# An output projection done as seven block products in place of eight, on one Trainium2 core

## The chip, the cores and the metric

One NeuronCore of a Trainium2 chip runs one launch of the kernel. The metric is device time in microseconds (us) for the whole step, of the slowest core, which here is the only one. Engines are named as in the profile: PE (TensorE) multiplies matrices, PEld is its weight load, DVE is VectorE, ACT is ScalarE, POOL is GpSimd, SP is SyncE, which only issues DMAs here. Weights are fetched by DMAs that ACT issues. Each engine works through its own instructions in the order in which they stand, and an instruction that waits holds up what stands behind it on its engine.

## The reference

One layer of a hybrid decoder. The prompt has 1024 tokens of width 2048, the decode samples are 8 x 8 = 64 tokens. One input projection gives the columns of 16 heads (6 mLSTM, 6 gated DeltaNet, 4 HGRN2, each 128 wide); each head runs a chunked recurrence; the results go through a norm per head and a gate, then through the output projection and a final norm:

```python
h = _rmsnorm(x, norm_w)
proj = jnp.einsum('bld,de->ble', h, w_in)
...
ha = jnp.concatenate(outs_a, axis=1) * jax.nn.sigmoid(heads(ao, H_A))
hb = jnp.concatenate(outs_b, axis=1)
hc = jnp.concatenate(outs_c, axis=1)
hcat = jnp.concatenate([ha, hb, hc], axis=2)
hcat = hcat * lax.rsqrt(jnp.mean(hcat * hcat, axis=-1, keepdims=True) + EPS)
y = hcat.reshape(bsz, L, MIX) * out_norm_w.astype(f32) * jax.nn.silu(z.astype(f32))
out = jnp.einsum('ble,ed->bld', y.astype(x.dtype), w_out)
return x + out, (st_a[0], st_a[1], st_a[2], st_b, new_conv, st_c)
```

The states of all heads are outputs too. The change touches `y @ w_out`, a product of 1024 (and 64) x 2048 by 2048 x 2048, what feeds it, and what follows it.

## The kernel before

The kernel works in two halves of the prompt, 512 tokens each; the samples ride along with the first. In each half it runs through the heads (`ORDER`). For each head it multiplies the columns of `w_in` with the normed and transposed x, which lies in SBUF in tiles `h00` to `h31`, and then starts the head's scan, its recurrence. These matmuls are called `acc` in the profile, those of the output projection `oacc`.

Products of fp32 precision are made of three fast ones. Every operand is split into `hi` (rounded) and `lo` (the rest), and the product is hi·hi + hi·lo + lo·hi. For weights this is done on the way: `feed_raw` has ACT issue the DMA of a 128 x 512 piece into `wraw` (5 buffers), `feed_split` has ACT cast it to `whi` and DVE subtract to `wlo` (4 buffers each), three pieces ahead of PE. For y, `finish` makes `hi` and `lo` at a head's end and stores both to `y_dram`.

The output projection (lines 1743 to 1802 of before) takes the first half's y from DRAM into the tiles `h..` (`load_y`), as soon as the last columns of the second half have been multiplied. It goes through 4 groups of 512 columns; in each through the 16 heads; and for each head's piece of weights through 4 tiles of 128 tokens (3 matmuls each), and a tile that holds `hi` and `lo` of the 64 samples (2 matmuls). Then it does the same for the second half, without samples. At the end of each group DVE adds the accumulators, which lie in PSUM banks (8 in all), to x; ACT sums squares; POOL multiplies by the final norm's weights. When a token tile has all four groups, `final_norm` scales it and SP stores it.

Work beside the matmuls is written as generators in queues (`scan`, `fin`, `post`, `bg`). `Weave.pump`, called after each handful of matmuls, takes the next step of a queue when its due time, by a rough clock in the code, has come. `drain_queue` steps all queues until the named one is empty, at once, at that point of the program:

```python
def drain(self, *streams):
    while any(not s.done for s in streams):
        heads = [q[0] for q in self.queues.values() if q]
        due = min(s.due for s in heads)
        self.clock.t["T"] = max(self.clock.t["T"], due)
        self.pump()
```

Names in the profile: `pan`, `pa`, `pkh`, `puh`, `poh` are the PE steps of an HGRN2 head's scan, in that order; `X`, `Ex`, `hkd`, `hqd` are made for it by POOL. The last head, C3, is such a one, and its scan runs into the output projection. `yd<-y` and `s<-yd` move y of a head through DRAM in `finish`; `Bb<-db` brings rows for the triangular solves of the gated DeltaNet heads.

Of the kernel before, what the change touches and what calls it, by code (L numbers as in the profile page):

```python
# [6 lines left out]
F32 = mybir.dt.float32  # L7
F32R = mybir.dt.float32r
# [5 lines left out]
P = 128  # L14
# [131 lines left out]
class Weave:  # L146
    def __init__(self, clock):
        self.clock = clock
        self.queues = {"scan": [], "fin": [], "post": [], "bg": []}
# [37 lines left out]
OUT_UNITS = ([(cg, range(5)) for cg in range(4)], [(cg, range(4)) for cg in range(3)] + [(3, range(2)), (3, range(2, 4))])  # L187
# [3 lines left out]
def hybrid_step(ctx, tc, i, o):  # L191
# [51 lines left out]
    def o_raw(k, cg):  # L243
        raw = wp.tile([P, 512], F32, tag="wraw", name="wraw", bufs=5)
        WDMA(raw, i["w_out"][0, P * k:P * (k + 1), 512 * cg:512 * (cg + 1)])
        return raw

# [95 lines left out]
    for units in OUT_UNITS:  # L343
        for cg, _ in units:
            for k in range(NK):
                pieces.append((o_raw, k, cg))
# [256 lines left out]
    y_dram = [dp.tile([NH, P, w], F32R, name=f"y{w}") for w in (2 * NSAMP + 2 * HALF, 2 * HALF)]  # L603
# [233 lines left out]

    def finish(half, head, outs, ssq, scale, zs):
# [30 lines left out]
        yield  # L869
        yhi, ylo = zs.bitcast(F32R), y.bitcast(F32R)  # L870
# [4 lines left out]
        d = y_dram[half.index][head].bitcast(F32)  # L875
        for part, t in enumerate((yhi, ylo)):
            t = t.bitcast(F32)
            at_ = 2 * NSAMP if half.first else 0
            DMA(d[:, at_ + HALF * part:at_ + HALF * (part + 1)], t[:, 0:HALF])
            if half.first:  # L880
                DMA(d[:, NSAMP * part:NSAMP * (part + 1)], t[:, HALF:WS])
# [90 lines left out]
    def mlstm_scan(half, h, kT, qT, vT, tho, zs, nm, em, st):  # L972
# [118 lines left out]
        weave.add("fin", finish(half, h, hxs, ssq, 0.25, zs))  # L1091
# [60 lines left out]
    def gdn_scan(half, h, ck_, cq, cv, zs, Gb, eG, bb, st):  # L1152
# [242 lines left out]
        weave.add("fin", finish(half, HA + h, hxs, ssq, 1.0, zs))  # L1395
# [22 lines left out]
    def hgrn_scan(half, h, kT, lf, qT, vT, zs, st):  # L1418
# [152 lines left out]
        weave.add("fin", finish(half, HA + HB + h, hxs, ssq, 0.25, zs))  # L1571
# [91 lines left out]
    def load_y(half, g):  # L1663
        w = y_dram[half.index].shape[-1]
        yT[half.index][g] = [hp.tile([P, 2, w], F32R, tag=f"h{g}{part}", name=f"y{g}{part}") for part in (0, 1)]
        for q in range(4):
            DMA(yT[half.index][g][q // 2][:, q % 2].bitcast(F32), y_dram[half.index][4 * g + q].bitcast(F32))

    def y_block(half, k, n, part):

        at_ = HALF * part + P * n
        return yT[half.index][k // 4][k % 4 // 2][:, k % 2, at_:at_ + P]

    hB, yT = {}, [{}, {}]
    for half, groups in zip(halves, group_lists):
# [4 lines left out]
        for n, group in enumerate(groups):  # L1680
# [5 lines left out]
            if half.first and n == 6:  # L1686
                weave.add("bg", prep_B())
            after = None
            if n == len(groups) - 1:
# [3 lines left out]
                else:  # L1693
                    after = lambda g: load_y(halves[0], g)
# [12 lines left out]

    ys_flat = o["y_sample"].rearrange("b t d -> (b t) d")
    tags = ["a", "b", "c", "d", "e", "f", "g", "h", "j", "a", "b", "c", "d", "e", "f", "g", "h", "j", "k", "u"]

    def final_norm(toks, some, res, ss, fr, late):
        for n in some:
            cnt = toks[n][1]
            V.tensor_reduce(fr[:cnt, n:n + 1], ss[:cnt, n], op=ALU.add, axis=AX.X)
            V.tensor_scalar(fr[:cnt, 8 + n:9 + n], fr[:cnt, n:n + 1], 1.0 / D, EPS, op0=ALU.mult, op1=ALU.add)
            G.tensor_tensor(fr[:cnt, 16 + n:17 + n], fr[:cnt, 8 + n:9 + n], halfneg[:cnt, 0:1], op=ALU.pow)
        yield
        for n in some:
            _, cnt, _, dst = toks[n]
            for cg in range(4):  # L1720
                t, r = res[n, cg], fr[:cnt, 16 + n:17 + n]
                if cg == 3 and late:
                    V.scalar_tensor_tensor(t[:cnt], t[:cnt], r, fnw[cg][:cnt], op0=ALU.mult, op1=ALU.mult)
                elif cg == 3 or late and cg == 2:
# [4 lines left out]
                yield  # L1729

# [12 lines left out]
    fnw = []  # L1743
    for half in halves:
        toks = []
        for n, (c0, cnt) in enumerate(half.tiles):
            if half.first and n == 0:
                toks.append((0, NSAMP, xs_flat, ys_flat))
            else:
                a = HALF * half.index + c0  # L1750
                toks.append((c0, P, i["x_prompt"][0, a:a + P], o["y_prompt"][0, a:a + P]))
        nt = len(toks)
        ss = sp.tile([P, 8, 4], F32, tag="oss", name="oss")
        fr = sp.tile([P, 24], F32, tag="fr", name="fr")
        res = {}
        for cg, some in OUT_UNITS[half.index]:
            ccols = slice(512 * cg, 512 * (cg + 1))
            accs = {n: bank("oacc") for n in some}
            for k in range(NK):
                whi, wlo = next_piece()  # L1760
                for n in some:
                    yh, yl = (y_block(half, k, n, part) for part in (0, 1))
                    both = toks[n][1] == NSAMP
                    T.matmul(accs[n], yh, whi, start=k == 0, stop=False)
                    T.matmul(accs[n], yh, wlo, start=False, stop=both and k == NK - 1)
                    if not both:
# [69 lines left out]
```

## Time and profile before

| what | value |
|---|---|
| median of 3 runs | 2499.4 us (2497.17 to 2501.01) |
| the profiled execution | 2499.9 us, its span 2498.2 us |
| granted TensorE clock | 0.991 |
| first `oacc` matmul of the output projection | 2097.5 us |
| HBM read, written | 285.71 MB, 62.19 MB |

Nearly all instructions are recorded under line 137, the line of a helper through which every engine call goes; so rows are told apart by their tiles, as `oacc<-whi,y`. "Busy" is the sum of an engine's instruction times. The chain of waits follows what ended last back to what released it. The rows that carry the argument stand in the prediction.

### The profile page before, as it was taken

The numbers are of one execution on the slowest core, as the hardware profiler recorded it, in microseconds if no ns is written. First come the engines' busy times: TensorE is split into PE (matmuls) and PEld (weight loads), VectorE is DVE, ScalarE is ACT, GpSimd is POOL, SyncE is SP. The second block draws the span as 40 slices with busy tenths as digits, with TensorE's granted clock in tenths as the row PEclk, the third lists the DMA queues.
The fourth block names the chain that finished last, engine by engine and source line by source line (L and its number), as shares of the span: only waits on it lengthen the run. The fifth ranks groups of instructions, "written<-read, shape, count | busy, mean of one in ns | idle before, by whom it ended". The sixth has DMA issues, their size and how long they took to land.

```text
span 2498.2 us, 43685 instructions
## 1 busy us (share of the span) xinstructions
PE 2437.1 (98%) x16032; PEld 2181.1 (87%) x16032; DVE 1441.9 (58%) x3080; ACT 993.4 (40%) x2428; POOL 548.7 (22%) x743
## 2 busy tenths in 40 slices
PE   6999999999999999999999999999999999999998
PEld 5999999999999999998787888888888888888886
DVE  7765766766647656556854556554654646333435
ACT  5643444443435334343642343343533334222324
POOL 5331211421204212113320113110310102111201
PEclk9999999999999999999999999999999999999999
DMA  6445756766645445348445445454544559526735
GB/s 138 111 119 144 175 131 135 187 147 159 147 108 142 99 119 146 93 112 244 112 121 123 112 120 135 118 134 98 144 118 112 132 124 307 135 84 201 252 100 181
DMA packets 681043, 350.81 MB, mean 140 GB/s; under 512 B 260004, under 2 KB 622076, under 8 KB 680828
## 3 DMA queue, kind: packets, MB, share of 16 engines
q10 hardware_dynamic: 318528, 185.64, 29.4%
q1 hardware_dynamic: 362300, 162.37, 24.9%
q8 instruction: 126, 2.06, 0.3%
q14 instruction: 89, 0.73, 0.1%
HBM read 285.71 MB, written 62.19 MB: 139 GB/s over the span
## 4 chain that ended last, share of the span: by engine, by line
PE 77%; DVE 8%; DMA 6%; issue 3%; ACT 2%; POOL 2%; SPq 1%; ACTq 0%; DVEq 0%; POOLq 0%
PE acc L137 53%; PE oacc L137 13%; DVE wlo L137 2%; DMA wraw<-in_w_in_dram 2%; PE pa L137 1%; PE po L137 1%; SPq L1209 1%; PE pyy L137 1%; PE nd L137 1%; DMA Bb<-db 1%; ACT whi L137 1%; PE pu L137 1%; PE pz L137 1%; DVE Yc L137 1%; DVE Yt L137 1%
## 5 line engine op out<-in xcount | busy, mean ns | idle before, releaser
L137 DVE TENSOR_TENSOR wlo<-wraw,whi 128x512 fp32r<-128x512 f32 x720 | 540.2, 752 | 552.5 <-ACT whi L137 534.7
L137 PE MATMUL acc<-hA,whi 128*128 128x288 f32 (+1 forms) x4544 | 819.6, 302 | 5.3 <-DVE whi L137 5.1
L137 ACT CAST whi<-wraw 128x512 fp32r<-128x512 f32 x720 | 443.9, 618 | 934.9 <-PE acc L137 427.5
L137 PE MATMUL acc<-hB,whi 128*128 128x512 f32 x2272 | 725.3, 401 | 3.6 <-DMA hB<-hblo 3.1
L137 PEld LDWEIGHTS acc<-hA,whi 128*128 128x128 f32 x4544 | 676.1, 190 | 10.2 <-issue 6.5
L137 PE MATMUL acc<-hA,wlo 128*128 128x288 f32 x2240 | 488.5, 298 | 4.7 <-DVE wlo L137 4.7
L137 PEld LDWEIGHTS acc<-hB,whi 128*128 128x128 f32 x2272 | 415.4, 190 | 85.6 <-DMA hB<-hblo 3.9
L137 PE MATMUL acc<-hB,wlo 128*128 128x512 f32 x1120 | 441.6, 394 | 1.5 <-DVE wlo L137 1.5
L137 PEld LDWEIGHTS acc<-hA,wlo 128*128 128x128 f32 x2240 | 365.7, 189 | 6.3 <-DVE wlo L137 6.3
L137 PE MATMUL oacc<-whi,y 128*128 128x512 f32 x1088 | 343.2, 390 | 0.0
L137 PEld LDWEIGHTS acc<-hB,wlo 128*128 128x128 f32 x1120 | 212.1, 189 | 49.4 <-DVE wlo L137 3.4
L137 PEld LDWEIGHTS oacc<-whi,y 128*128 128x128 f32 x1088 | 204.3, 188 | 42.8 <-ACT whi L137 0.8
L137 PE MATMUL oacc<-wlo,y 128*128 128x512 f32 x576 | 224.6, 390 | 2.0 <-DVE wlo L137 2.0
L137 PEld LDWEIGHTS oacc<-wlo,y 128*128 128x128 f32 x576 | 108.2, 188 | 25.4 <-DVE wlo L137 3.3
L137 POOL TENSOR_TENSOR res<-res,fnw 128x512 f32<-128x512 f32 (+1 forms) x34 | 48.6, 1460 | 258.5 <-ACT oscr L137 258.5
L137 POOL TENSOR_TENSOR y<-y,zs 128x592 fp32r<-128x592 f32 (+1 forms) x32 | 46.1, 1441 | 153.2 <-ACT zs L137 138.9
L137 POOL TENSOR_TENSOR qd<-qT,emb 128x512 f32<-128x512 f32 x12 | 16.9, 1404 | 219.1 <-PE po L137 219.0
L137 DVE TENSOR_TENSOR Yt<-Yc,Bb 128x60 f32<-128x60 f32 (+8 forms) x180 | 36.5, 203 | 47.5 <-DMA Bb<-db 42.4
L137 POOL TENSOR_TENSOR hr<-hr,halfneg 128x4 f32<-128x4 f32 (+1 forms) x48 | 44.7, 931 | 70.3 <-DVE hr L137 69.3
L137 POOL TENSOR_TENSOR nrm<-nrm,halfneg 128x10 f32<-128x10 f32 x12 | 24.0, 1998 | 125.0 <-DVE nrm L137 125.0
L137 POOL TENSOR_TENSOR X<-Ex,hk 128x256 f32<-128x256 f32 (+1 forms) x40 | 39.7, 992 | 52.4 <-PE pa L137 40.7
L137 DVE TENSOR_TENSOR Sx<-Sx,lf 128x256 f32<-128x256 f32 (+2 forms) x60 | 35.3, 590 | 20.8 <-ACT Ex L137 18.9
(416 smaller groups left out, 2748.4 us busy)
## 6 DMA issues: line engine op xcount, KB each, us to landing
wraw<-in_w_in_dram ACTq DMA_DIRECT2D x564, 256.0 KB
wraw<-in_w_out_dram ACTq DMA_DIRECT2D x144, 256.0 KB
y<-y SPq DMA_DIRECT2D x16, 576.0 KB
px<-in_x_prompt_dram SPq DMA_DIRECT2D x32, 256.0 KB
yd<-y SPq DMA_DIRECT2D x128, 64.0 KB
out_dram<-sst SPq DMA_DIRECT2D x16, 512.0 KB
s<-yd SPq DMA_DIRECT2D x32, 256.0 KB
y<-zs SPq DMA_DIRECT2D x32, 256.0 KB
```

What stands on the lines that cost most here:

```text
L137: return f(out, *a, **k)
L1209: DMA(db[j], Ball[SUB * j:SUB * (j + 1), 0:C, SUB * j:SUB * (j + 1)])
```

## The change

The output projection of the prompt becomes one level of Strassen's scheme, in Winograd's form. Call the two token halves' y over the first 8 heads (`K1`) and the last 8 heads (`K2`) A11, A12 (first half) and A21, A22 (second half), and the quarters of `w_out` B11, B12 (rows of K1; columns 0 and 1, columns 2 and 3 of 512) and B21, B22 (rows of K2). In place of eight products of quarters there are seven, in this order, each over 8 heads and both of its column groups (`phase` is one column group of one product):

1. A11·B11. 2. A12·B21. 3. S2·T2. 4. S4·B22. 5. S1·T1. 6. S3·T3. 7. A22·T4.

Here S1 = A21 + A22, S2 = S1 - A11, S3 = A11 - A21, S4 = A12 - S2, T1 = B12 - B11, T3 = B22 - B12, T2 = B22 - T1, T4 = B21 - T2. The samples are multiplied as before, with the plain pieces of weights: beside products 1, 2 and 4, and in product 3 with 16 pieces of their own.

**Sums of weights.** `combine_weights`, a generator in a new queue `mix`, starts behind the second half's preparation (`prep_B`). For each of 16 groups SP loads four pieces into the tiles `px` and `pxs`, POOL makes four subtractions in place, SP stores four sums (T1 to T4) to DRAM. On SP the four loads and four stores of a group stand next to each other, or with a few rows of others between.

**The second half's y** is stored whole (`y_whole`), not as `hi` and `lo`: 16 casts on ACT, 16 subtractions on POOL and 16 stores go.

**Sums of y.** `fill` loads y of the second half (`beside`, three buffers deep), has POOL and DVE make the operand of a later product, from it and from what lies in the tiles, and has ACT cast `hi` and DVE subtract `lo` into the tile just read. Product 6 loads A11 a second time.

**Accumulators.** A product's sum is kept (`t1`, `q`) and added to by POOL or DVE, with x, until a row is complete. After the first column group of product 1, ACT copies four accumulators into `t1`, whose tiles are `px` and `pxs`, behind `weave.drain_queue("mix")`.

```diff
+HEADS = [{"A": 0, "B": HA, "C": HA + HB}[name[0]] + int(name[1]) for name in ORDER[1:]]
+K1, K2 = HEADS[:NH // 2], HEADS[NH // 2:]
+LAST_UNITS = [(0, range(4)), (1, range(2)), (1, range(2, 4))]
...
+        if not half.first:
+            DMA(y_whole[head], y[:, 0:HALF])
+            return
         yhi, ylo = zs.bitcast(F32R), y.bitcast(F32R)
         S.copy(yhi[:, 0:W], y[:, 0:W])
         yield
         G.tensor_tensor(ylo[:, 0:W], y[:, 0:W], yhi[:, 0:W], op=ALU.subtract)
...
+    def combine_weights():
+        while not prep_stream.done:
+            yield
+        for j in range(2):
+            for kk in range(NK // 2):
+                b11, b12, b21 = (sp.tile([P, 512], F32, tag="px", name="px", bufs=3) for _ in range(3))
+                b22 = sp.tile([P, 512], F32, tag="pxs", name="pxs", bufs=1)
+                for t, heads, cg in ((b11, K1, j), (b12, K1, j + 2), (b22, K2, j + 2), (b21, K2, j)):
+                    tc.keep_in_program_order(DMA(t, i["w_out"][0, P * heads[kk]:P * (heads[kk] + 1), 512 * cg:512 * (cg + 1)]))
+                for dst, a, b in ((b11, b12, b11), (b12, b22, b12), (b22, b22, b11), (b21, b21, b22)):
+                    ck.last = ck.t["T"] + 9.0
+                    yield
+                    G.tensor_tensor(dst, a, b, op=ALU.subtract)
+                ck.last = ck.t["T"] + 20.0
+                yield
+                for n, t in (("T1", b11), ("T3", b12), ("T2", b22), ("T4", b21)):
+                    DMA(w_comb[n][NK // 2 * j + kk], t)
+                    ck.last = ck.t["T"] + 3.0
+                    yield
...
+    def phase(u, j, accs, tiles, own=None, other=None, each=()):
+        for kk in range(NK // 2):
+            whi, wlo = next_piece()
+            for n in tiles:
+                yh, yl = (y_block(u, kk, n, part) for part in (0, 1))
+                T.matmul(accs[n], yh, whi, start=kk == 0, stop=False)
+                T.matmul(accs[n], yh, wlo, start=False, stop=False)
+                T.matmul(accs[n], yl, whi, start=False, stop=kk == NK // 2 - 1)
...
+    def fill(u, loads, ops, again=None):
+        for kk in range(NK // 2 + 2):
+            if kk > 1:
+                hi, lo = parts(u, kk - 2)
+                src = beside[0][(kk - 2) % 3]
                 ck.begin()
+                S.copy(hi, src)
+                ck.sync()
+                V.tensor_tensor(lo, src, hi, op=ALU.subtract)
+            if kk < NK // 2:
+                for x, heads in enumerate(loads):
+                    weave.drain(fins[1, heads[kk]])
+                    DMA(beside[x][kk % 3], y_whole[heads[kk]])
...
+    for j in range(2):
+        accs, sacc = banks(), bank("oacc")
+        phase(0, j, accs, halfn, own=(sacc, samples(0)))
+        if j == 0:
+            weave.drain_queue("mix")
+            ck.begin()
+            for n in halfn:
+                t1[j, n] = sp.tile([P, 512], F32, tag="px" if n < 3 else "pxs", name="t1", bufs=3 if n < 3 else 1)
+                S.copy(t1[j, n], accs[n])
...
+    fill_with(0, [K1, K2], [(G, 0, 1, PLUS), (V, 0, ("hi", 0), LESS), (V, 0, ("lo", 0), LESS)])
...
+    fill_with(1, [], [(G, ("hi", 1), ("lo", 1), PLUS), (G, 0, ("hi", 0), LESS), (G, 0, ("lo", 0), LESS)])
...
+    fill_with(0, [K1, K2], [(G, 0, 1, PLUS)])
...
+    fill_with(1, [K1], [(G, ("hi", 1), 0, LESS), (G, 0, ("lo", 1), PLUS)], again=K1)
...
+    fill_with(0, [K2], [])
```

How the instructions then stand, at the place where the scan of the last head runs into the output projection. On PE before, from the transposes of `hkd` on, behind the 173rd `oacc` matmul (`y_23925` is a tile of y):

```order
L137 MATMUL pkh<-ident,hkd 128x128 x4
L137 MATMUL oacc<-whi,y_23925 128x512
L137 MATMUL oacc<-wlo,y_23925 128x512
L137 MATMUL oacc<-whi,y_23925 128x512 x2
L137 MATMUL oacc<-wlo,y_23925 128x512
L137 MATMUL oacc<-whi,y_23925 128x512
L137 MATMUL puh<-s_24304,s_24342 128x128 x4
```

On PE after the change, the same steps and the last of `pa` ahead of them, behind the 112th, which is the last of the first column group of product 1:

```order
L137 MATMUL pa<-X_24400 32x32 x2
L137 MATMUL pa<-Ex 32x64 x2
L137 MATMUL pkh<-ident,hkd 128x128 x4
L137 MATMUL puh<-s_24443,s_24458 128x128 x4
L137 MATMUL poh<-state_C_766,hqd 128x128
L137 MATMUL poh<-s_24443,AT 128x128
L137 MATMUL oacc<-whi,y_23834 128x512
L137 MATMUL poh<-s_24460,hqd 128x128
```

The `oacc` matmuls that stood between the scan's steps have moved behind them, all but one.

On POOL, where the operands of these steps are made, before:

```order
L137 TENSOR_TENSOR Ex<-Ex,hq 128x4x64
L137 TENSOR_TENSOR X_24221<-Ex,hk 128x8x32
L137 TENSOR_TENSOR X_24221<-Ex,hq 128x8x32
L137 TENSOR_TENSOR hkd<-Sx,hk 128x512
L137 TENSOR_TENSOR hqd<-eP,hq 128x512
```

and after (`px` and `pxs` are the last group of weight sums, `t_24515` to `t_24521` the four tiles of `t1`):

```order
L137 TENSOR_TENSOR Ex<-Ex,hq 128x4x64
L137 TENSOR_TENSOR px<-px 128x512
L137 TENSOR_TENSOR px<-pxs,px 128x512
L137 TENSOR_TENSOR pxs<-pxs,px 128x512
L137 TENSOR_TENSOR px<-px,pxs 128x512
L137 TENSOR_TENSOR X_24400<-Ex,hk 128x8x32
L137 TENSOR_TENSOR X_24400<-Ex,hq 128x8x32
L137 TENSOR_TENSOR hkd<-Sx,hk 128x512
L137 TENSOR_TENSOR res<-res,t_24515 128x512
L137 TENSOR_TENSOR res<-res,t_24517 128x512
```

The four sums have come in ahead of `X` and `hkd`, and additions of `t1` ahead of `hqd`, which follows after two more.

On ACT after the change, the copies into `t1` and the copy of `pkh` that `puh` needs (before, that copy stood between two weight pieces, with no copy of accumulators near it):

```order
L137 COPY t_24515<-oacc 128x512
L247 DMA wraw<-in_w_out_dram 128x512
L137 COPY t_24517<-oacc 128x512
L137 COPY t_24519<-oacc 128x512
L137 COPY t_24521<-oacc 128x512
L137 CAST whi<-wraw 128x512
L247 DMA wraw<-in_w_out_dram 128x512
L137 COPY oscr<-oacc 64x512
L137 COPY s_24458<-pkh 128x512
L137 COPY s_24480<-poh 128x512
```

The scan's two copies now stand behind the four of `t1`, which need the tiles that the last group of weight sums is stored from.

More of the change, by code (lines that the diff above doesn't have):

```diff
@@ L1090, in mlstm_scan @@
         G.tensor_copy(Cn, last)
-        weave.add("fin", finish(half, h, hxs, ssq, 0.25, zs))
+        add_finish(half, h, hxs, ssq, 0.25, zs)
         if not half.first:
@@ L1729, in final_norm @@
                 yield
+            free.extend(res.pop((n, cg)) for cg in order)
     def norm_states():
```

343 lines of the change are left out of this document (250 added, 93 removed).

## The prediction

> **What bounds the kernel now.** I read the engine shares of the page first, then the table of stretches through the output projection, then the chain of waits there.
>
> ```profile
> span 2498.2 us, 43685 instructions
> PE 2437.1 (98%) x16032; PEld 2181.1 (87%) x16032; DVE 1441.9 (58%) x3080; ACT 993.4 (40%) x2428; POOL 548.7 (22%) x743
> ...
> L137 PE MATMUL oacc<-whi,y 128*128 128x512 f32 x1088 | 343.2, 390 | 0.0
> ...
> L137 PE MATMUL oacc<-wlo,y 128*128 128x512 f32 x576 | 224.6, 390 | 2.0 <-DVE wlo L137 2.0
> ```
>
> PE works 98% of the span, and the 1088 + 576 = 1664 matmuls of the output projection (`oacc`) waited 2.0 us in all. The stretches say the same (length, then busy time of PE, PEld, DVE, ACT and POOL with counts, granted clock, DMA share, GB/s):
>
> ```profile
> 2100.00:2120.00 20.00, 20.00 (x96) 16.90 (x95) 16.49 (x25) 9.73 (x21) 11.39 (x13) 1.00 0.96 309
> ...
> 2200.00:2240.00 40.00, 40.00 (x179) 33.11 (x178) 14.15 (x19) 11.15 (x23) 7.25 (x5) 1.00 0.29 81
> ...
> 2320.00:2360.00 40.00, 39.77 (x175) 32.45 (x174) 17.00 (x32) 13.55 (x25) 3.21 (x3) 1.00 0.94 321
> ```
>
> Even where DMA is busy 0.94 to 0.96 of the time, PE does not starve. DVE and POOL have much room in the middle of the stage. So a matmul fewer here is time saved, for as long as the others keep up.
>
> ```profile
> 2097.54 15.87 PE oacc L137 x70
> 2113.40 1.30 PE pan L137 x8
> ...
> 2117.91 0.89 PE pa L137 x8
> ...
> 2136.56 1.71 PE pa L137 x34
> ...
> 2142.80 0.44 PE pkh L137 x4
> ...
> 2144.62 0.91 PE puh L137 x8
> ...
> 2147.39 1.78 PE poh L137 x16
> ...
> 2158.26 149.21 PE oacc L137 x658
> ```
>
> This is the chain of waits (start, length, what). Two things to see: an `oacc` matmul costs 149.21 / 658 = 0.2268 us, and the last head's scan (`pan` to `poh`) is spread thinly between `oacc` pieces, so that its waits are covered.
>
> **Term A, matmuls: -43.5 us.** Before, the prompt takes 4 column groups x 16 heads x 8 token tiles x 3 = 1536, the samples 128. After, seven products x 2 column groups x 8 heads x 4 tiles x 3 = 1344, the samples 128 again. So 192 go: 192 x 0.2268 = 43.5 us. Eight of 144 weight pieces go too; their splits were hidden, so they count nothing.
>
> **Term B, the weight sums under the two halves: +5 us.** They add 64 POOL subtractions; 16 heads lose one POOL subtraction and one ACT cast each.
>
> ```profile
> 2310.21 5.06 POOL L137 TENSOR_TENSOR res<-res,fnw 128x512 f32<-128x512 f32 x4 [43.53 <-ACT oscr L137]
> ...
> L137 POOL TENSOR_TENSOR y<-y,zs 128x592 fp32r<-128x592 f32 (+1 forms) x32 | 46.1, 1441 | 153.2 <-ACT zs L137 138.9
> ...
> 600.00:800.00 200.00, 200.00 (x1641) 197.07 (x1640) 127.13 (x299) 86.43 (x236) 49.20 (x73) 1.00 0.57 137
> ...
> 1200.00:1400.00 200.00, 196.05 (x1065) 161.06 (x1064) 125.61 (x245) 84.99 (x187) 43.01 (x49) 0.99 0.51 125
> ...
> 1800.00:2000.00 200.00, 198.93 (x1095) 165.38 (x1094) 113.40 (x225) 74.85 (x183) 35.20 (x39) 0.99 0.49 120
> ...
> L650 SPq DMA_DIRECT2D hbhi<-px x64: 302/482/1766, 285.5 to 672.3; - x64
> ```
>
> A POOL operation of this size takes 5.06 / 4 = 1.27 us: 64 x 1.27 = 81, less 16 x 1.44 = 23, is 58 us more POOL. The sums begin when the second half's preparation is through (its last store is at 672) and end with the main stage near 2100, so 8 us fall into each 200. That lifts POOL from 35 to about 43. Rows that busy show PE idle between 0 (600 to 800) and 3.95 (1200 to 1400), against 1.07 at 35. So the ends are 0 and (3.95 - 1.07) x 7.2 = 21 us over 1430 us. I take 5: the row with the most POOL lost nothing, and its load of DVE is that of the bad row.
>
> **Term C, the last head's scan laid bare: +10 us.** The order rows above show it. The code drains the weight-sum queue after the first column group, and with it everything left of the scan is written in front of the second. On PE the fourth `pa`, `pkh`, `puh` and `poh` now stand behind `oacc` number 112 with one matmul among them. PE gets there at 2097.54 + 112 x 0.2268 + 1.30 + 3 x 0.89 = 2126.9; its own work there is 1.71 + 0.44 + 0.91 + 1.78 = 4.84 us. The rest is waiting:
>
> ```profile
> 2143.74 0.59 ACT L137 COPY s<-pkh 128x512 f32<-128x512 f32 x1 [1.41 <-PE pkh L137]
> ...
> 2145.96 1.11 DVE L137 SCALAR_TENSOR_TENSOR s<-s,eP,puh 128x128 f32<-128x128 f32 x3
> ...
> 2114.27 0.38 SPq L816 DMA_DIRECT2D s<-hvT  x1
> 2114.69 3.58 SPq L1788 DMA_DIRECT2D res<-in_x_prompt_dram  x4
> ...
> 2326.49 5.35 DMA out_dram<-res
> ...
> 2337.25 5.83 DMA res<-in_x_prompt_dram
> ```
>
> At best `pkh` to `puh` costs 1.09 us for the copy (2143.24 to 2144.33) and `puh` to `poh` 1.54 for DVE (2145.53 to 2147.07): PE idle 2.6 us, the low end. But on POOL the last group's four subtractions stand ahead of `hkd`, and on ACT four copies into the tiles of that same group stand ahead of the copy of `pkh`; those wait until the group's stores have landed. SP issues its four loads behind `s<-hvT`, as it issues four others now, until 2118.3. With 5.83 to land and 4 x 1.27 the sums are done at 2129, the last store at 2129 + 5.4 = 2134.6. Then four copies, a cast, a copy of the samples and that of `pkh` on ACT (the last four 0.6 each, 2.4), `puh`, 1.54 and `poh`: 2141. Without waits PE would be through at 2126.9 + 4.84 = 2131.7. So I take 10. If load and store take twice as long, since DMA is at 0.96 up to 2120, it is 10 + 11 = 21, the high end.
>
> **Term D, operands made in the output stage: +7 us.** POOL gets 56 sums there and 32 additions (x and partial products) beside its 34 products with the norm's weights; DVE gets 16 subtractions and 40 `lo` parts.
>
> ```profile
> 2308.10 0.68 DVE L137 TENSOR_TENSOR wlo<-wraw,whi 128x512 fp32r<-128x512 f32 x1
> 2308.70 0.67 DVE L137 TENSOR_TENSOR res<-res,oacc 128x512 f32<-128x512 f32 x1
> ...
> 2309.90 1.87 DVE L137 TENSOR_TENSOR res<-res,oacc 128x512 f32<-128x512 f32 x3
> ...
> 2318.32 1.70 DVE L137 TENSOR_TENSOR wlo<-wraw,whi 128x512 fp32r<-128x512 f32 x1
> ...
> 2317.29 2.18 POOL L137 TENSOR_TENSOR res<-res,fnw 128x512 f32<-128x512 f32 x1
> ```
>
> A `wlo` takes 0.60 us (start to start) alone, and 1.70 while POOL runs, which itself then takes 2.18 and not 1.27; additions that read an accumulator keep their 0.62 beside POOL (2309.90). So POOL and DVE's subtractions are to be added up. In the second product PE has 224 x 0.2268 = 50.8 us; POOL has the 24 operations of the third operand, 8 additions and 8 products, 40 x 1.27 = 50.8, and DVE 32 (16 `wlo`, 10 `lo`, 6 sums) x 0.60 = 19.2: over by 19.2. In the fifth, PE has 192 x 0.2268 = 43.5; POOL 32 (16 sums, 8 products, 8 additions) x 1.27 = 40.6, DVE 24 (16 `wlo`, 8 `lo`) x 0.60 = 14.4: over by 11.5. Elsewhere there is room. High end 31, low end 0, if neighbours and the three pieces split ahead (about 9 us) take it all. I take 7, since both cover most of each.
>
> DVE's first four subtractions stand eight pieces ahead of the first output piece and wait there for the first load of y.
>
> ```profile
> 2063.69 2.20 SPq L1667 DMA_DIRECT2D y<-y  x4
> ```
>
> Issued by 2065.9 and landed 5.83 later, at 2071.7; DVE gets there with PE eleven pieces of 12 x 0.2268 = 2.72 us before 2097.54, at 2067.6. It waits 4 us; three pieces split ahead, 8.2 us, cover that: 0.
>
> [...]
>
> The final norms, stores and the tail keep their form; their weights still arrive late at the end, and I count nothing.
>
> **Sum.** The profiled execution took 2499.9 us (span 2498.2 and 1.7 around it), 0.5 above the median of the three runs. 2499.9 - 43.5 + 5 + 10 + 7 = 2478.4; I predict 2478.
>
> **Rivals.**
>
> All is hidden: B and D at 0, C at 2.6 gives 2459. For it: DVE and POOL stand idle in most rows. Against: the drain's order is fixed.
>
> Sums do not overlap: POOL and DVE add up strictly, D is 31, 2502, with 2490 to 2506 around it. For it: the 1.70. Against: over the whole output stage the two have (122 x 1.27 + 192 x 0.60) = 270 us for 1472 x 0.2268 = 334, so queues can even out.
>
> SP as a new brake, slower: each of the 16 weight groups puts four stores behind four loads on SP, which stands still for up to 5.35 + 4 x 1.27 = 10.4 us.
>
> ```profile
> DVE Yt L137 <- DMA Bb<-db: 42.4, 12, 5.3
> ```
>
> Behind it wait the rows that the solves need; DVE waits for those 42.4 / 12 = 3.5 us a time already. If each group adds as much on PE, 16 x 3.5 = 56 in place of B's 5 gives 2529. It is slower than before from (21.5 + 5.0 + 5) / 16 = 2.0 us a group. Against: in the second half PE idles about 1 us in 200 (1800 to 2000, above), so these waits are mostly covered, and what stands right behind the stores is seldom a row for a solve.
>
> No effect: 32 pieces of weights in the third product leave 1.6 us a piece, and weights take over the pace there and elsewhere: 2500.
>
> ```profile
> 2471.49 6.49 DMA wraw<-in_w_out_dram
> ```
>
> Five buffers cover 5 x 1.6 = 8 us against 6.49 for a late piece now: not likely.
>
> **Chances.** Forecast 0.56 (2464 to 2490), all hidden 0.15, no overlap 0.16, SP 0.10, no effect 0.03. A measurement of this kernel can tell about 0.2%, 5.0 us, from no change. The no-overlap case splits into 0.06 faster, 0.07 same, 0.03 slower: faster 0.56 + 0.15 + 0.06 = 0.77, same 0.10, slower 0.13. The range 2458 to 2497 leaves out SP, and the upper part of no overlap.
>
> **What would show it.** A: 1472 `oacc` matmuls at 0.227 us. B: PE idle per 200 us between 700 and 2100 up by less than 1. C: one PE gap near 2130, before `pkh` or `puh`, of about 10 us, released by ACT or POOL behind DMA. D: short PE waits for `wlo` or `whi` in the second, third and fifth product, with ACT's casts of `y` waiting for POOL. If C's gap is missing, or the main stage grows by over 20 us, the prediction is wrong in its middle.

## The result, and the profile after

| | before | after |
|---|---|---|
| median of 5 runs | 2501.0 us (2497.2 to 2507.9) | 2523.0 us (2521.1 to 2534.7) |
| ratio, 95% interval | | 1.0091 (1.0061 to 1.0120) |
| span of the profiled execution | 2498.2 us | 2519.3 us |
| last `hbhi` store (end of the second half's preparation) | 672.3 us | 677.1 us |
| first `oacc` | 2097.5 us | 2123.6 us |

The kernel became slower by 0.9%, where 0.9% faster was forecast. The page of the changed kernel, its engine shares and the two groups of `oacc`:

```profile
span 2519.3 us, 43946 instructions
PE 2409.7 (96%) x15840; PEld 2152.8 (85%) x15840; DVE 1559.8 (62%) x3170; ACT 1006.1 (40%) x2458; POOL 750.0 (30%) x879
...
L137 PE MATMUL oacc<-whi,y 128*128 128x512 f32 x960 | 308.9, 396 | 10.0 <-DVE res L137 6.9
...
L137 PE MATMUL oacc<-wlo,y 128*128 128x512 f32 x512 | 203.5, 397 | 7.6 <-DVE wlo L137 7.4
```

The 192 matmuls are gone (960 + 512 = 1472). But their mean grew from 390 to 396 ns and they now wait 10.0 + 7.6 us, where they had waited 2.0. The stretches (same columns as in the prediction) show where, and that the main stage lost time too:

```profile
1600.00:1640.00 40.00, 33.01 (x210) 26.67 (x209) 21.97 (x55) 9.28 (x19) 8.07 (x9) 0.87 0.58 158
1800.00:2000.00 200.00, 193.12 (x1050) 160.32 (x1049) 119.90 (x220) 73.64 (x174) 51.21 (x54) 0.97 0.56 144
...
2140.00:2180.00 40.00, 29.02 (x179) 25.10 (x178) 17.96 (x31) 12.14 (x28) 19.04 (x18) 0.87 0.60 184
2240.00:2280.00 40.00, 36.84 (x148) 29.37 (x147) 31.30 (x30) 17.48 (x36) 31.56 (x20) 0.91 0.50 149
2320.00:2360.00 40.00, 40.00 (x178) 33.14 (x177) 18.81 (x23) 10.24 (x17) 14.92 (x11) 1.00 0.55 177
2360.00:2400.00 40.00, 35.35 (x145) 28.33 (x144) 25.66 (x36) 15.56 (x32) 23.62 (x17) 0.91 0.57 178
```

Two things go together in each bad row: PE idle, and a granted clock under 1.00. So each stage is accounted for in three parts, from windows of 5 us: PE's idle time; the time lost to the clock (PE's busy time x (1 - granted clock), summed); and the rest, which is work at full clock.

| stage | kernel | length | PE idle | lost to clock | rest |
|---|---|---|---|---|---|
| last `hbhi` store to first `oacc` | before | 1425.2 | 15.7 | 7.9 | 1401.6 |
| | after | 1446.6 | 33.0 | 11.9 | 1401.7 |
| first to last `oacc` | before | 390.0 | 2.0 | 0.0 | 388.0 |
| | after | 384.8 | 28.6 | 8.5 | 347.7 |

The work itself came out as planned: the same in the main stage, 40 us less in the output stage. Idle time and clock took back 21 and 35. The beginning, up to the `hbhi` store, is the same program; its 4.9 us are chance (672 to 680 in all profiles here). 4.9 + 21.4 - 5.2 = 21.1, the difference of the spans.

**The main stage.** The longest of its waits, on the timelines of PE, DVE and POOL (start, length, what, and in brackets the idle time before it):

```profile
1630.18 1.35 PE L137 MATMUL pz<-X,Ball 32*32 32x32 f32 x32 [6.99 <-DVE X L137]
```

```profile
1623.80 0.17 DVE L137 TENSOR_TENSOR Yt<-Yc,Bb 128x16 f32<-128x16 f32 x1
1624.01 0.17 DVE L137 TENSOR_TENSOR Yc<-Yc,Yt 128x16 f32<-128x16 f32 x1
1624.22 1.38 DVE L137 TENSOR_TENSOR Yt<-Yc,Bb 128x12 f32<-128x12 f32 x1
1625.64 0.17 DVE L137 TENSOR_TENSOR Yc<-Yc,Yt 128x12 f32<-128x12 f32 x1
1625.84 1.12 DVE L137 TENSOR_TENSOR Yt<-Yc,Bb 128x8 f32<-128x8 f32 x1
...
1627.19 1.11 DVE L137 TENSOR_TENSOR Yt<-Yc,Bb 128x4 f32<-128x4 f32 x1
...
1628.54 1.24 DVE L137 TENSOR_TENSOR Y<-Yc,evenodd 128x128 f32<-128x128 f32 x1
```

```profile
1624.31 1.26 POOL L137 TENSOR_TENSOR px<-px 128x512 f32<-128x512 f32 x1
1625.65 1.28 POOL L137 TENSOR_TENSOR px<-pxs,px 128x512 f32<-128x512 f32 x1
1627.01 1.27 POOL L137 TENSOR_TENSOR pxs<-pxs,px 128x512 f32<-128x512 f32 x1
1628.37 1.27 POOL L137 TENSOR_TENSOR px<-px,pxs 128x512 f32<-128x512 f32 x1
```

DVE works through a triangular solve, a chain of small operations on two SBUF tiles, 0.17 us each. Beside each of POOL's four subtractions one of them takes 1.1 to 1.4. That adds (1.38 + 1.12 + 1.11 - 3 x 0.17) + (1.24 - 0.29) = 4.1 us to the solve (0.29 is the `Y` step in a4, with nothing on POOL), just at its end, where PE is already waiting. The same happened at 1924.8, with 6.9 us.

**The output stage.** The chain of waits in it:

```profile
2141.41 7.04 DMA pxs<-in_w_out_dram
...
2148.64 1.29 POOL px L137
...
2152.62 1.43 POOL X L137 x2
...
2154.72 3.88 DMA res<-in_x_prompt_dram
...
2159.98 1.27 POOL yb L137
...
2164.60 0.69 DVE res L137
2165.31 0.58 ACT oscr L137
2165.92 0.59 ACT s L137
...
2166.55 2.08 PE puh L137 x8
```

```profile
2166.55 2.08 PE L137 MATMUL puh<-s,s 128*128 128x128 f32 x8 [10.56 <-ACT s L137]
```

PE waited 10.6 us there for `s`, the copy of `pkh`. The first half of the chain is the one that the prediction named: loads, `px` sums, then `X`. The second half is not: x's rows for an addition on POOL, the first operand sum `yb` behind it, and DVE and ACT behind that. Then the second product:

```profile
2249.16 3.32 POOL L137 TENSOR_TENSOR yb<-yb,y 128x512 f32<-128x512 f32 x2
2252.44 1.29 POOL L137 TENSOR_TENSOR yb<-y 128x512 f32<-128x512 f32 x1
2253.81 3.26 POOL L137 TENSOR_TENSOR yb<-yb,y 128x512 f32<-128x512 f32 x2
```

```profile
2253.18 1.10 DVE L137 TENSOR_TENSOR y<-yb,y 128x512 fp32r<-128x512 f32 x1 [1.84 <-ACT y L137]
2254.20 1.75 DVE L137 TENSOR_TENSOR wlo<-wraw,whi 128x512 fp32r<-128x512 f32 x1
2255.87 3.06 DVE L137 TENSOR_TENSOR res<-res,oacc 128x512 f32<-128x512 f32 x5
```

```profile
2256.60 0.80 PE L137 MATMUL oacc<-whi,y 128*128 128x512 f32 x1 [3.16 <-DVE res L137]
```

From 2232.9 to 2259.6 POOL goes without a pause, and where a DVE subtraction of this size runs beside it both are longer: a sum 1.65 in place of 1.27, `wlo` 1.67 from start to start in place of 0.60. DVE reaches the accumulators late, the banks come free late, and PE waits 3.16 us at 2256.6. At 2366.7 it is 3.74; there POOL's sums wait for the second load of A11 besides.

### The profile page after: what moved, and what is told of

Its sections match the earlier page's. It is cut to its first block, busy times and chain, and to the rows that moved or that the text cites. A ratio compares the mean times of both kernels' runs of the same rounds, so it can differ in the third digit from the quotient of the medians.

```text
span 2519.3 us, 43946 instructions
## 1 busy us (share of the span) xinstructions
PE 2409.7 (96%) x15840; PEld 2152.8 (85%) x15840; DVE 1559.8 (62%) x3170; ACT 1006.1 (40%) x2458; POOL 750.0 (30%) x879
## 4 chain that ended last, share of the span: by engine, by line
PE 65%; DVE 13%; DMA 8%; POOL 5%; issue 4%; ACT 3%; SPq 2%; ACTq 1%; DVEq 0%; POOLq 0%
PE acc L137 48%; PE oacc L137 6%; DVE wlo L137 3%; POOL yb L137 2%; DVE Yt L137 1%; PE pa L137 1%; PE po L137 1%; DMA Bb<-db 1%; ACT whi L137 1%; SPq L1243 1%; PE pyy L137 1%; DVE Yc L137 1%; PE nd L137 1%; PE pz L137 1%; DMA wraw<-in_w_in_dram 1%
## 5 line engine op out<-in xcount | busy, mean ns | idle before, releaser
L137 DVE TENSOR_TENSOR wlo<-wraw,whi 128x512 fp32r<-128x512 f32 x712 | 562.2, 792 | 408.5 <-ACT whi L137 387.8
L137 ACT CAST whi<-wraw 128x512 fp32r<-128x512 f32 x712 | 437.8, 617 | 838.6 <-PE acc L137 403.9
L137 PEld LDWEIGHTS acc<-hA,wlo 128*128 128x128 f32 x2240 | 365.2, 189 | 12.3 <-DVE wlo L137 12.3
L137 PE MATMUL oacc<-whi,y 128*128 128x512 f32 x960 | 308.9, 396 | 10.0 <-DVE res L137 6.9
L137 PEld LDWEIGHTS oacc<-whi,y 128*128 128x128 f32 x960 | 183.9, 192 | 50.0 <-DVE res L137 7.8
L137 PE MATMUL oacc<-wlo,y 128*128 128x512 f32 x512 | 203.5, 397 | 7.6 <-DVE wlo L137 7.4
L137 PEld LDWEIGHTS oacc<-wlo,y 128*128 128x128 f32 x512 | 97.7, 191 | 31.8 <-DVE wlo L137 11.8
L137 DVE TENSOR_TENSOR Yt<-Yc,Bb 128x60 f32<-128x60 f32 (+8 forms) x180 | 43.2, 240 | 50.4 <-DMA Bb<-db 45.1
L137 DVE TENSOR_TENSOR y<-yb,y 128x512 fp32r<-128x512 f32 x40 | 37.4, 936 | 37.0 <-ACT y L137 36.9
L137 DVE TENSOR_TENSOR s<-s,hr 128x512 f32<-128x512 f32 x32 | 28.0, 876 | 43.3 <-POOL hr L137 43.3
L137 ACT CAST y<-yb 128x512 fp32r<-128x512 f32 x40 | 24.8, 620 | 73.5 <-POOL yb L137 37.5
```

The lines of the kernel that those rows point to most:

```text
L137: return f(out, *a, **k)
```

## The experiments

"Main" is the stretch from the last `hbhi` store to the first `oacc`, "output" that from first to last `oacc`. Medians are set against runs of before on the same chip, 2503 to 2504 us.

| run | median us | ratio (95%) | main | output | PE idle, lost to clock in output |
|---|---|---|---|---|---|
| a1_mix_on_dve | 2500.1 | 0.9988 (0.9970 to 1.0006) | 1430.4 | 384.8 | 29.3, 7.9 |
| a2_mix_sooner | 2501.0 | 0.9998 (0.9982 to 1.0013) | 1435.0 | 378.0 | 23.7, 5.5 |
| a3_fill_on_dve | 2512.2 | 1.0029 (1.0015 to 1.0042) | 1456.1 | 370.4 | 19.2, 6.0 |
| a4_all_three | 2495.6 | 0.9961 (0.9945 to 0.9978) | 1446.0 | 363.8 | 12.3, 5.3 |
| b1_no_subtraction | 2495.7 | 0.9964 (0.9951 to 0.9976) | 1418.5 | 387.5 | 32.2, 8.3 |
| b2_pool_only | 2549.7 | 1.0186 (1.0171 to 1.0201) | 1475.3 | 384.9 | 26.2, 11.3 |
| b3_gaps | 2513.3 (one run) | | 1421.2 | 400.4 | 9.8, 1.7 |
| b4_late_drain | 2487.7 | 0.9938 (0.9921 to 0.9954) | 1427.5 | 370.7 | 20.1, 3.5 |
| c1_products_alone | 2453.3 | 0.9805 (0.9776 to 0.9834) | 1415.8 | 346.1 | 2.4, 0.0 |
| c2_no_operand_sums | 2509.1 | 1.0027 (1.0009 to 1.0045) | 1448.9 | 368.7 | 15.8, 7.3 |
| c3_tail_faster | 2484.9 | 0.9927 (0.9904 to 0.9951) | 1422.6 | 374.4 | 19.9, 6.9 |

The same program gives "main" within some 5 us of itself either way: 1425.2 and 1421.2 for that of before, 1446.6, 1456.1 and 1448.9 for that of the change.

**a1_mix_on_dve: the weight sums on DVE**

```diff
-                    G.tensor_tensor(dst, a, b, op=ALU.subtract)
+                    V.tensor_tensor(dst, a, b, op=ALU.subtract)
```

> The changed kernel with one edit: the 64 subtractions of the weight sums stand on DVE in place of POOL; loads, stores, their pacing and all else stay. In the changed kernel the first oacc comes at 2123.7 us, 21 later than the 4.8 of the common beginning explain. Theory L (lock): while a POOL subtraction of 1.27 us runs, DVE's small operations of the solve (0.17 us) take 1.1 to 1.4; four in a row stretch a solve, and PE waits 7.0 us for X twice, with matmuls at half speed behind it. Then this edit takes back most of it: first oacc at 2102 to 2112, no wait of PE for X over 3 us, total near 2510. Rival S (SP and DMA): the four loads and four stores of each group hold up the rows of the solves. Then nothing changes up to the first oacc (2118 or later), total near 2523. Rival V: DVE stands waiting for the loads instead, since they are now in its own queue: first oacc after 2124.

The main stage fell from 1446.6 to 1430.4, the first `oacc` came at 2104.5, and the longest wait for `X` was 1.7 us. The solve's groups, of the change and of a1:

```profile
L137 DVE TENSOR_TENSOR Yt<-Yc,Bb 128x60 f32<-128x60 f32 (+8 forms) x180 | 43.2, 240 | 50.4 <-DMA Bb<-db 45.1
```

```profile
L137 DVE TENSOR_TENSOR Yt<-Yc,Bb 128x60 f32<-128x60 f32 (+8 forms) x180 | 36.8, 205 | 49.9 <-DMA Bb<-db 44.8
```

The operations went back to 205 ns (203 before), though DVE has 64 operations more; the waits for the DMA `Bb<-db`, which the SP rival lives on, stayed (45.1 and 44.8). L holds, S and V fall here; the total, 2500, came out lower than the 2510 expected.

**a2_mix_sooner: the last weight group ends before the output stage**

```diff
-                    ck.last = ck.t["T"] + 9.0
+                    ck.last = ck.t["T"] + 8.0
...
-                ck.last = ck.t["T"] + 20.0
+                ck.last = ck.t["T"] + 18.0
```

> The changed kernel with the pacing of the weight groups shortened (9.0 to 8.0 and 20 to 18 in the table of due times), so that the last group ends inside the second half and the drain after the first column group of product 1 finds nothing to do; the last head's scan then stands between oacc matmuls again. Theory (drain): the PE idle of 10.9 us between 2140 and 2180 and the slow matmuls behind it (granted clock 0.74 there) go: first to last oacc shorter by 12 to 16 us, total near 2509, if the main stage stays; the sums hit other solves there, so its end may move by 10 either way. Rival: the scan waits for its own chain (state, X) whatever stands between: PE idle there stays above 7 us.

The output stage got shorter by 6.8 us, half of what was expected. The scan stands between `oacc` matmuls again, and PE's wait before `puh` fell from 10.6 to 3.7; what is left of it waits for ACT, which had casts of operands ahead. The main stage moved too (1435.0), since the same sums met other solves.

**a3_fill_on_dve: the operand sums on DVE**

```diff
-    fill_with(0, [K1, K2], [(G, 0, 1, PLUS), (V, 0, ("hi", 0), LESS), (V, 0, ("lo", 0), LESS)])
+    fill_with(0, [K1, K2], [(V, 0, 1, PLUS), (V, 0, ("hi", 0), LESS), (V, 0, ("lo", 0), LESS)])
```

(and the same for the other three calls)

> The changed kernel with the operand sums of the output stage (56 on POOL) moved to DVE; POOL keeps the additions of x and of partial products and the products with the norm's weights. Up to product 2 the program is the same. Theory L (POOL and DVE's subtractions shut each other out): of the 17.5 us that PE waits after 2185 (for wlo, res and whi) some 12 go, with the slow matmuls behind them, since a sum costs DVE 0.6 in place of 1.27 of both: total near 2507. Rival W (the waits come from the additions at the end of each column group and the x loads): PE still waits over 12 us after 2185, total 2518 or more. Rival V: DVE, now with 56 x 0.6 = 34 us more, becomes late with wlo: slower than 2523.

The output stage fell by 14.4 us to 370.4. The total fell less than expected, 2512 for 2507, as this profile's main stage was one of the long ones. DVE in the second product, with nothing on POOL beside it:

```profile
2248.07 0.68 DVE L137 TENSOR_TENSOR y<-yb,y 128x512 fp32r<-128x512 f32 x1
2248.68 0.68 DVE L137 TENSOR_TENSOR wlo<-wraw,whi 128x512 fp32r<-128x512 f32 x1
2249.28 0.69 DVE L137 TENSOR_TENSOR yb<-yb,y 128x512 f32<-128x512 f32 x1
```

All three sorts now take 0.6 us from start to start. One engine does in 0.6 each what two engines did in 1.65 and 1.67 beside one another. The wait before `puh` stayed at 10.0 us: the first sum now stands in DVE's queue and waits there for its own load of y.

**a4_all_three: a1, a2 and a3 together**

> The three edits together: weight sums on DVE, shorter pacing, operand sums on DVE. If the three theories hold (L in the main stage about 15 us, drain about 14, L in the output stage about 15) the total is 2479 or thereabouts, faster than before by 0.9 per cent; if only the drain matters 2509; if none, 2520 to 2525.

The output stage came out at 363.8, shorter than the change's by 21.0; 14.4 + 6.8 = 21.2, so the two edits there add up. But the main stage was 1446.0, as long as the change's, with sums on DVE. With the shorter pacing the four sums of a group fell into another solve, at 913.4 to 917.4; they cost it their own time on DVE and a wait of 1.36 us for their load, and PE waited 3.4 us for `X` at 921.9. Where the sums fall counts, on whichever engine they are: with the same pacing and the weight sums on POOL (a2) main was 1435.0, shorter than here. The medians agree, since a4 is only 5.4 us below a2 with an output stage shorter by 14.2. So DVE was the better place for the weight sums at the pacing of the change, and not at this one. The total, 2495.6, missed the expected 2479 for the most part by that stage.

**b1_no_subtraction: loads and stores alone**

```diff
-                    G.tensor_tensor(dst, a, b, op=ALU.subtract)
```

> The changed kernel with the 64 subtractions of the weight sums left out; the loads and the stores of the 16 groups stay, so the four T arrays hold plain weights and the prompt's outputs are not the reference's. Measured on the stretch from the last hbhi store to the first oacc: 1425.2 us before, 1446.5 in the changed kernel. Theory L (a POOL subtraction holds up DVE's small operations in the solves): it falls to 1425 to 1435 and PE no longer waits over 3 us for X. Rival S (the loads and stores on SP and the DMA engines): it stays at 1440 or more.

1418.5: all of the main stage's loss came from the 64 subtractions. The 64 loads and 64 stores cost it nothing that can be seen. S falls. In the output stage PE still waited 11.6 us before `puh`, without a single subtraction of weights. DVE there:

```profile
2136.10 1.73 DVE L137 TENSOR_TENSOR yb<-yb,y 128x512 f32<-128x512 f32 x1 [9.28 <-POOL yb L137]
```

So it is not the four `px` sums that make the wait at `puh` long, but the first operand sum, `yb`, which came late on POOL behind an addition that waited 5.62 us for x's rows. SP issued those rows right behind the group's last store (2124.73), and the chain of waits shows how long they took:

```profile
2125.63 7.80 DMA res<-in_x_prompt_dram
```

**b2_pool_only: subtractions alone**

```diff
-                    DMA(w_comb[n][NK // 2 * j + kk], t)
```

(with the loads of 15 of the 16 groups, and c_raw taking plain weights)

> The counterpart: all 64 subtractions on POOL, on the tiles that the first group loads; the other 15 groups of loads and all stores are left out, and the products take plain weights instead of the four T arrays, so the prompt's outputs are not the reference's. Theory L: the stretch from the last hbhi store to the first oacc stays long, 1438 to 1456 us, and the trace shows DVE operations of the solve at over 1 us beside POOL's subtractions. Rival S: 1425 to 1432, as before. After the first column group the t1 copies no longer wait for stores: if C is the chain behind loads and stores, PE's wait there falls from 10.6 us to under 5.

With no load to wait for, the 64 subtractions ran almost without a pause, from 687 to 779 us, across one head's solve. It is the plainest picture of what one engine does to the other (DVE, then POOL):

```profile
719.07 1.31 DVE L137 TENSOR_TENSOR Yc<-Yc,Yt 128x55 f32<-128x55 f32 x1
720.41 1.30 DVE L137 TENSOR_TENSOR Yt<-Yc,Bb 128x50 f32<-128x50 f32 x1
```

```profile
719.04 1.27 POOL L137 TENSOR_TENSOR pxs<-pxs,px 128x512 f32<-128x512 f32 x1
720.39 1.26 POOL L137 TENSOR_TENSOR px<-px,pxs 128x512 f32<-128x512 f32 x1
```

DVE makes one step per POOL operation here: 1.3 us for steps that took 0.21 on average in before. PE waited 23 us twice, and main was 1475, over the expected 1456, because the sums stood elsewhere than in the change. The wait before `puh` was 4.1 us, as expected of C without its loads and stores; at this place b2 has neither transfers nor subtractions, since these were over by 779. As b1 with the transfers alone had 11.6, the transfers are part of that chain, the subtractions hardly.

**b3_gaps: waits of PE made on purpose**

```diff
+                if k == 9 and cg < 3:
+                    gap_bank = bank("gap")
+                    T.transpose(gap_bank[:, 0:P], ident, ident)
+                    a_, b_ = sq("io", "gap"), sq("io", "gap")
+                    S.copy(a_, gap_bank[:, 0:P])
+                    for x in range(GAPS[half.index, cg]):
+                        S.copy(*((b_, a_) if x % 2 == 0 else (a_, b_)))
```

> The kernel of before with six made waits in its output projection: at the tenth weight piece of six column groups PE transposes a tile, ACT copies it 1 + 1, 3, 6, 10, 15 or 22 times over, and PE transposes the copy before it goes on; nothing else is added. It measures what a wait of PE costs beside its length. In the traces so far PE's granted clock stands at 0.50 for 6 to 14 us behind waits of 3 us and more, which costs another 3 to 7 us. Theory K (a threshold): waits under about 2 us leave the clock at 1.00, waits over about 4 us are each followed by a stretch at 0.50 of much the same length, whatever the wait's length. Rival P (in proportion): the slow stretch grows with the wait, and short waits have a short one. Total by K: 2500 + the six waits (about 1, 1.5, 2.5, 3.5, 5, 7) + 3 x 5 = 2535.

A miss for the most part: at five of the six places the order as built put other `oacc` matmuls ahead of the waiting transpose, and PE waited at one only, for 8.29 us:

```profile
2349.00:2352.00 3.00, 0.00 (x0) 0.00 (x0) 0.26 (x1) 1.67 (x6) 0.00 (x0) 0.99 1.01 295
2352.00:2355.00 3.00, 0.00 (x0) 0.00 (x0) 0.43 (x1) 0.86 (x4) 0.00 (x0) 0.50 1.04 388
2355.00:2358.00 3.00, 2.68 (x7) 2.19 (x8) 0.69 (x1) 0.79 (x2) 0.00 (x0) 0.50 0.97 331
2358.00:2361.00 3.00, 3.00 (x13) 2.41 (x13) 0.56 (x1) 0.62 (x1) 0.00 (x0) 0.88 0.29 98
```

The clock falls to 0.50 inside the wait and stays there until some 3.4 us after work has begun again; the loss was 1.7 us, less than the 3 to 7 expected. One wait can't tell K (a threshold) from P (in proportion); the last section looks at the waits of the other runs.

**b4_late_drain: sums on DVE, the drain moved**

```diff
-            weave.drain_queue("mix")
             ck.begin()
             for n in halfn:
-                t1[j, n] = sp.tile([P, 512], F32, tag="px" if n < 3 else "pxs", name="t1", bufs=3 if n < 3 else 1)
+                t1[j, n] = early[n]
...
     weave.drain_queue("scan")
+    weave.drain_queue("mix")
```

(with `early` from the tiles of `sst` and `vx`, and the operand sums in `px` and `pxs`)

> The changed kernel with both sorts of sums on DVE, the pacing of the weight groups as in the change, and the drain of the weight sums moved behind the second column group of product 1: the first four partial products go to tiles that lie free (those of sst and vx) and not to the tiles of the weight sums, which the operand sums use later in their place. If the theories hold, the main stage is that of a1 (1430 us from last hbhi store to first oacc) and the output stage that of a4 (364 us): 674 + 1430 + 364 + 12 = 2480, faster than before by 0.9 per cent. Rival: the long main stage of a4 (1446) comes from DVE's sums themselves and not from the pacing: 2495.

Faster than before by 0.6% (0.9938, 0.9921 to 0.9954). The main stage was 1427.5, as expected, so a4's long one came from its pacing. The output stage was 370.7 and not 364: 4.9 us of waiting before `puh` are left, behind casts of operands on ACT. The total, 2487.7, lies midway between the expected 2480 and the rival's 2495.

**c1_products_alone: the seven products without sums**

> The changed kernel with its seven products alone: the weight sums (loads, subtractions, stores) and the making of the operands (loads, sums, casts of y) are left out, the products take plain weights and y as it lies, so the prompt's outputs are not the reference's. It measures term A and, by difference, all that B, C and D cost together. If A is 192 x 0.2268 = 43.5 us and the waits come from the sums and their transfers: main stage 1418 to 1425 us from last hbhi store to first oacc, output stage (first to last oacc) 345 to 353 against 390.0 before, total 2456 to 2464. Rival: the order of the products brings waits of its own (additions of partial products, x loads): output stage over 360, total over 2470.

```profile
L137 PE MATMUL oacc<-whi,y 128*128 128x512 f32 x960 | 303.0, 390 | 0.0
...
L137 PE MATMUL oacc<-wlo,y 128*128 128x512 f32 x512 | 199.7, 390 | 2.4 <-DVE wlo L137 2.2
```

2453.3. The matmuls are back at 390 ns, the output stage is 390.0 - 346.1 = 43.9 us shorter than before, and no wait comes from the order of the products. Against the changed kernel's 2523.0, making and moving the operands costs 70 us.

**c2_no_operand_sums: the output stage without POOL's 56 sums**

> The changed kernel with the 56 POOL sums of the output stage left out (not moved): loads of y, casts and lo parts stay, so the prompt's outputs are not the reference's. Main stage as in the change (1446 to 1456). Output stage: 384.8 in the change, 370.4 with these sums on DVE. Theory L: POOL's sums cost PE by shutting out DVE's subtractions and by coming late for ACT's casts; without them 365 to 372, no better than on DVE by more than 5. Rival W: most of the waits after 2185 belong to the additions at the ends of the column groups: over 378.

368.7, shorter than the change's by 16.1. On DVE (a3) the same sums left the stage at 370.4, only 1.7 above this. So nearly the whole price of these sums is that they stand on POOL. What is left over c1's 346.1, 22.6 us, is mostly C's: PE still waits 1.9, 4.9 and 2.9 us at `pa`, `puh` and `poh`, 9.7 in all beside the change's 10.6, with slow clock behind them.

**c3_tail_faster: b4 with the last four weight groups sooner**

```diff
+                late = j == 1 and kk >= 4
...
-                    ck.last = ck.t["T"] + 9.0
+                    ck.last = ck.t["T"] + (7.0 if late else 9.0)
...
-                ck.last = ck.t["T"] + 20.0
+                ck.last = ck.t["T"] + (14.0 if late else 20.0)
```

> The kernel with both sorts of sums on DVE and the late drain, with shorter due times (7 for 9, 14 for 20) for the last four of the 16 weight groups alone, so that the last group's stores are over before the output stage while the other twelve stay where they were. Theory: PE's wait of 4.9 us for the copy of pkh goes, output stage from 370.7 to about 364, main stage stays at 1425 to 1432: total 2480. Rival: the four groups now meet the solve near 1900 or the last heads, and the main stage grows by what the output stage gains: 2488.

No gain that shows: 2484.9 with 0.9927 (0.9904 to 0.9951), beside 0.9938 for b4; the output stage was 374.4, where 364 was expected. The wait before `puh` fell to 2.8 us, but one of 4.8 before `pa`, for DVE's `AT`, took its place. DVE, which now makes all sums, is what the last scan meets.

## Why the prediction was wrong

The sum was 2499.9 - 43.5 + 5 + 10 + 7. Measured, by the spans: -43.9 (c1) + 21.4 in the main stage + 38.7 in the output stage (384.8 against c1's 346.1) + 4.9 of chance at the beginning = +21.1.

**A, right.** 43.5 forecast, 43.9 measured.

**B, the step that failed: +5 forecast, +21.4 measured.** The prediction read the cost of 64 more POOL operations from how POOL's busy time and PE's idle time go together in stretches of 200 us, and took the row with the most POOL, which lost nothing, as the likeliest. The trace of before has other rows with about as much POOL, which the prediction did not use, and they lost time:

```profile
800.00:1000.00 200.00, 197.62 (x1629) 193.15 (x1629) 120.76 (x286) 76.25 (x215) 48.83 (x73) 1.00 0.49 123
1000.00:1200.00 200.00, 192.95 (x1510) 183.17 (x1508) 115.23 (x269) 80.58 (x210) 46.17 (x53) 0.98 0.54 144
```

So PE's idle time was 0.0, 2.4 and 7.1 us in three rows with POOL at 46 to 49 (the last of them holds the passage between the two halves too). An average over 200 us doesn't hold what matters: which DVE operation stands beside which POOL operation. The fact was in the prediction, under D: `wlo` 0.60 alone and 1.70 beside POOL. It was used for the output stage and not for the solves, where operations of 0.17 us with two SBUF tiles took 1.1 to 1.4 beside POOL's 1.27 (1624 to 1630 of the change). a1 and b1 show it from both sides: main was 1430.4 with the subtractions on DVE and 1418.5 without them. The high end of B, 21, was the right size, for another reason; what it would have taken is the timeline of one solve, and the question what four operations of 1.27 us do to it.

**C, right in place and size (10 forecast, 10.6 waited), half right in cause.** The drain did lay the scan bare, and loads and sums stood ahead of `X`. But b1 kept the wait without those sums: the longer branch goes through the first operand sum, late on POOL behind x's addition (in a3, late on DVE behind its load), and from there through DVE and ACT to the copy of `pkh`. The wait fell to about 4 us where the weight groups' transfers were gone (b2) or out of the way (a2). Without the operand sums (c2) it split into three waits of 9.7 us together, so these sums are the last link of the chain and not its main cause; that the size fitted is in part luck. What the change, b1 and c2 have in common there are the group's loads and stores on SP, with x's rows behind them, for which POOL's additions wait; that the place of x's rows alone makes the wait is not shown.

**D, mis-sized: +7 forecast.** C and D together took 38.7 where 17 was forecast. Without the 56 sums the stage is 16.1 us shorter (c2), more than twice the 7; the rest, 22.6, is mostly C's waits and slow clock. The step "neighbours cover most" failed: POOL was busy for 53.4 us between 2190 and 2257 with 34 operations, where 50.8 us for 40 were worked out, since a sum beside DVE's subtractions took 1.65 and not 1.27. That DVE's operations are held up beside POOL's is plainest in b2, where steps of 0.21 us took 1.3 beside POOL's 1.27; what holds them up, no run tests. Added up strictly, D was 31, and 16.1 was measured.

**What no term held: the clock.** The waits themselves rose by (33.0 - 15.7) + (28.6 - 2.0) = 43.9 us, the time lost to the clock by (11.9 - 7.9) + 8.5 = 12.5 more. All waits were priced by their length alone.

**The rivals.** "Sums do not overlap" (2502) had what b2 shows, 1.3 us a step beside POOL's 1.27, and put it in one stage only. "SP as a new brake" (2529) had nearly the right time by the wrong mechanism: b1 rules it out for the main stage, where it was put. "All is hidden" and "No effect" fall with the waits shown above. The mark set in advance, a main stage longer by over 20 us, was met.

**Both kernels beaten.** b4 and c3, the change with all sums on DVE and the drain moved, are faster than before by 0.6 to 0.7%; of c1's 1.95% that is a third.

## What to carry to other kernels

Before work is put on POOL because POOL is idle, look at what DVE does at those moments: a chain of small operations with two SBUF operands paid up to one whole POOL operation per step here (b2: 1.3 us for steps of 0.21), and the busy shares of the kernel before don't show it. A sum that takes DVE 0.6 us was cheaper there, on the busier engine, than on POOL, in the output stage (a3) and, at the pacing of the change, in the main stage (a1); a2 and a4 show that another pacing can turn this round. Price a long wait of PE above its length: here the four of over 2.5 us in the table below, 3.16 to 8.29, were followed by another 1.7 to 3.9 us lost to the clock.

## What was not expected of the hardware

Behind short waits of PE the granted clock fell to 0.50 at some places: behind 1.86 us at 2411.3 of the change it did, behind 1.61 at 2213.2 it did not. For some of the waits of over 0.8 us, the time lost to the clock within 20 us behind each, from windows of 2 us:

| kernel, at us | PE waited | lost to clock |
|---|---|---|
| after, 2213.2 | 1.61 | 0.0 |
| after, 2411.3 | 1.86 | 1.7 |
| a3, 2264.6 | 2.36 | 0.0 |
| before, 1323.0 | 2.42 | 1.7 |
| after, 2256.6 | 3.16 | 3.1 |
| after, 2366.7 | 3.74 | 2.6 |
| after, 1630.2 | 6.99 | 3.9 |
| b3, 2355.3 | 8.29 | 1.7 |
| before, 1901.7, next to 32 x 32 matmuls | 0.94 | 1.7 |
| b3, 1906.0, the same place | 0.93 | 0.0 |
| a3, 1455.2 and 1457.8, between them 32 x 32 matmuls | 1.05 and 0.88 | 6.8 |
| a2, 1455.8 and 1458.4, the same place | 1.00 and 0.88 | 0.0 |

The loss does not follow the wait's length. It often is 1.7 or near 3.4, and behind the waits of up to 2.4 us it came at some and not at others. In windows of 0.5 us the clock stands at 0.50 for 3.4 us from 1325.5 and from 1902.4 of before and from 2412.9 of the change, for 6.8 from 2255.9 and from 2365.1, and for 10.2 from 1627.8; the loss is half of the time in which PE works there. Theory K's bounds of 2 and 4 us were a guess, and these rows don't bear them out: at 2411.3 a wait of 1.86 us between full-size matmuls was followed by 3.4 us at 0.50. The last four rows are two places of the program, each in two runs: the same short waits cost nothing in one run and 1.7 or 6.8 us in another. In a3 some 14 us at 0.50 came behind them:

```profile
1460.00:1463.00 3.00, 3.00 (x8) 1.98 (x6) 0.85 (x3) 0.00 (x0) 0.87 (x2) 0.50 0.92 167
...
1466.00:1469.00 3.00, 3.00 (x30) 2.09 (x29) 1.54 (x4) 0.00 (x0) 0.00 (x0) 0.50 0.35 80
```

So the length of a wait alone doesn't tell its price. What decides between the two runs of a place, no run here tests.
